# A list-scheduled transformer block on one core: the planner learns PSUM banks and a VectorE-GpSimd lock, norm1's gain goes into w_in, freed buffers are passed on, the second norm is done in halves, and the first MLP splits join the plan

## The chip, the cores and the metric

The kernel runs on one core of a Trainium2 chip. Its time is device microseconds of one execution; the time before is the median of three, 1164.03 us (1163.81 to 1168.68).

## What is computed

One block of a hybrid transformer in float32, on 1024 tokens of width 1024:

```python
h = rms_norm(x, norm1_g)
proj = h @ w_in                               # [1024, 1024] x [1024, 2560]
q, k, v, xl, gl = split(proj)                 # five parts of 512
q, k = rms_norm of each head (8 heads of 64), with q_norm_g, k_norm_g
attn = stick_breaking_attention(q, k, v)      # per 128 rows; a product of (1 - sigmoid z) over later keys
xl = causal_depthwise_conv(xl)                # 4 taps
lru = rg_lru(xl) * gelu(gl)                   # two 64x64 block gates, then a linear recurrence over time
x = x + concat(attn, lru) @ w_out             # [1024, 1024] x [1024, 1024]
h = rms_norm(x, norm2_g)
x = x + square(relu(h @ w_up)) @ w_down       # 1024 -> 4096 -> 1024
```

## The kernel before

**Products.** Every large product is three matmuls: each operand is split into a high part, rounded to fp32r, and a low part, the rest (high by a copy, low by a subtraction), and low x high, high x low and high x high are summed in PSUM. So each operand of TensorE passes two other engines first.

**Two stages.** The front holds everything up to the second norm, 0 to about 533 us of the profile. The MLP behind it multiplies 2x2 blocks with seven products in place of eight, in a sequence written out by hand (`up_group`, `down_group`, L980 is the helper that issues all of it); the change touches only its first few splits.

**The front's order** is not written by hand. `record_front` (L370 and on) records operations as `op(engine, cost in ns, function, reads, writes)`, grouped in units: X (transpose two 128-row tiles of x, `xt`, and split them into `hTh`, `hTl`), S (mean square of x), C (small vectors), W (load 128x256 blocks of w_in, `wrq`/`wrv`/`wrl`, and split them into `wq`, `wv`, `wl`), Q, V, L (projections, `pq`, `pv`, `pxl`, `pgl`, and what follows them: `ss`, `qv`, `rb` are the head norms), A and D (attention of a pair of heads and 256 rows: scores `z`, `G` the scan, `w` the weights, `pw` their transposes, `wt` their split, `av` the product), B (blocks of w_out, `ro`, split into `wo`), M (blocks of the mixer's output, `rm`, split into `mx`), O and U (product `po`, added to `x1`), H (second norm: transpose x1, `ht`, times norm2_g into `h2`; squares `jh`). The string `ORDER` gives the units' priorities. `Plan.schedule` then runs an event-driven list schedule over PE, DVE, ACT, POOL and SP with the given costs, and what it finds is the order in which each engine's instructions are issued (`Pinned` holds them to it; all are issued from L859). Its costs before are round: 900 ns for a VectorE low part of 128x512, 1400 to 1500 ns for a GpSimd operation of that shape; it lets any two engines read one PSUM bank at once, and lets VectorE and GpSimd run beside each other.

**Buffers.** `COUNT` gives the slots per tag. `CLOSES`/`OPENS` say which tags end before others begin, since they take the same memory: x1, wo, mx and r2 (the buffers of B, M, O and U) open only when the last user of w, wr, lg, f, hT, rsb and bd is done; h2 opens when attention is done. In program order, the loads of B50 and B40 come first in `ORDER` but wait for that.

**The hand-over.** After the plan `mlp_head()` issues the splits of the first MLP operands (`m0b` from h2, `sb` from w_up), and the first four MLP products are not held to program order (`PINNED = 4`).

Of the kernel before, what the change touches and what calls it, by code (L numbers as in the profile page):

```python
# [10 lines left out]
F32 = mybir.dt.float32  # L11
F32R = mybir.dt.float32r
# [8 lines left out]
P = 128  # L21
# [29 lines left out]
PTAGS = ("z", "pd", "pw", "av")  # L51

MM = {512: 227, 384: 173, 256: 117, 128: 109}
WIN = 3413.0
KEEP = {"PE": 0, "DVE": -77, "ACT": -95, "POOL": -40, "SP": 0}


def dve(n):
    return 210 + 0.93 * n


def dve2(n):
    return 230 + 1.45 * n


def act(n):
    return 185 + 0.82 * n


def gps(n):  # L70
    return 350 + 1.95 * n


class V:
    def __init__(self, plan, tag, name):
        self.plan, self.tag, self.name = plan, tag, name
        self.wr, self.rd, self.real = {}, {}, None
        self.slot, self.ops, self.allocs = None, {}, []
        self.left = None
# [10 lines left out]
class Op:  # L90
    __slots__ = ("eng", "cost", "fn", "deps", "succ", "prio", "set", "grp", "nd", "ready", "start", "end", "unit", "kb", "what", "tiles", "n", "as_", "ae", "work", "closes")


class Plan:
    def __init__(self):
        self.ops, self.queue, self.unit = [], {}, 0
        self.groups = {}
# [4 lines left out]
    def op(self, eng, cost, fn, r=(), w=(), set=None, grp=None, kb=0, what="", work=None):  # L102
        o = Op()
        o.work = work
# [26 lines left out]
        for acc in r:  # L131
            v, sub = acc if isinstance(acc, tuple) else (acc, None)
            v.rd.setdefault(sub, []).append(o)
            v.ops[o] = 1
        deps.pop(o, None)
# [29 lines left out]
    def schedule(self):  # L165
# [3 lines left out]
        dma_free = 0.0  # L169
# [35 lines left out]
        while len(done) < n:  # L205
# [68 lines left out]
            else:  # L274
                o.end = s + cost
# [4 lines left out]
            for q in o.succ:  # L280
                lat = 0 if q.eng == e and e != "SP" else 150 if q.eng == "POOL" else 50
# [6 lines left out]
            for v in o.tiles:  # L288
                v.left -= 1
                v.end = max(v.end, o.end)  # L290
                if not v.left:
                    k, q = nxt[v.tag], self.queue[v.tag]
                    if k < len(q):
                        nxt[v.tag] = k + 1
                        alloc(q[k], v.slot, v.end + 50)
            for k in o.closes:
                left[k] -= 1
                late[k] = max(late[k], o.end)
                if not left[k]:
                    for tag in OPENS[k]:  # L300
# [17 lines left out]
def record_front(plan, E, order):  # L318
# [4 lines left out]
    bd = V(plan, None, "bd")  # L323
# [8 lines left out]

    def const0():
        E.grow = plan.tile("lg", "grow")
        g = E.grow
        op("SP", 0, lambda: E.sp.dma_start(g[:NT, 0:P], E.norm1_g.rearrange("o (c p) -> (o c) p", p=P)), w=[g], kb=4)
        pg = plan.tile("pd", "pg1")
        op("PE", 260, lambda: E.pe.transpose(pg[:, 0:NT], g[:NT, 0:P], E.ident[:NT, :NT]), r=[g], w=[pg], what="gain")
        op("DVE", 170, lambda: E.dve.tensor_copy(E.gain1, pg[:, 0:NT]), r=[pg], w=[gain1], what="gain")

    def const1():
        vr = plan.tile("lg", "vrow")

        def loads():
            E.sp.dma_start(vr[0:16, 0:P], E.conv_w.rearrange("o k (c p) -> (o k c) p", p=P))
            for i, v in enumerate((E.conv_b, E.b_rg, E.b_ig, E.lam)):
                E.sp.dma_start(vr[16 + 4 * i:20 + 4 * i, 0:P], v.rearrange("o (c p) -> (o c) p", p=P))
            E.sp.dma_start(vr[32:40, 0:P], E.norm2_g.rearrange("o (c p) -> (o c) p", p=P))
            for i, v in enumerate((E.q_norm_g, E.k_norm_g)):
                for h in range(2):  # L350
                    E.sp.dma_start(vr[40 + i:41 + i, HD * h:HD * h + HD], v)
        op("SP", 10, loads, w=[vr], kb=30)
        pv = plan.tile("pd", "pv")
        op("PE", 260, lambda: E.pe.transpose(pv[:, 0:42], vr[:42, 0:P], E.ident[:42, :42]), r=[vr], w=[pv], what="vec")
        op("DVE", 200, lambda: E.dve.tensor_copy(E.vec, pv[:, 0:42]), r=[pv], w=[vec], what="vec")
        op("DVE", 200, lambda: E.dve.scalar_tensor_tensor(E.gcol, E.vec[:, 40:41], 1.0 / math.sqrt(HD), E.vec[:, 41:42], op0=ALU.mult, op1=ALU.mult),
           r=[vec], w=[gcol])
        lm = lambda: E.vec[:, 28:32]
        ta, tb, tc_ = (V(plan, None, n) for n in ("ta", "tb", "tc"))
        op("DVE", 200, lambda: E.dve.tensor_scalar_mul(E.t_a, lm(), -1.0), r=[vec], w=[ta])  # L360
        op("DVE", 200, lambda: E.dve.tensor_tensor(E.t_b, lm(), E.t_a, op=ALU.max), r=[vec, ta], w=[tb])
        op("ACT", 200, lambda: E.act.activation(E.t_b, E.t_b, AF.Sigmoid, scale=-1.0), r=[tb], w=[tb], set="sig")
        op("DVE", 200, lambda: E.dve.tensor_scalar(E.t_c, E.t_b, -1.0, 2.0, op0=ALU.mult, op1=ALU.add), r=[tb], w=[tc_])
        op("DVE", 200, lambda: E.dve.reciprocal(E.t_c, E.t_c), r=[tc_], w=[tc_])
        op("DVE", 200, lambda: E.dve.tensor_tensor(E.t_b, E.t_b, E.t_c, op=ALU.mult), r=[tb, tc_], w=[tb])
        op("DVE", 200, lambda: E.dve.tensor_tensor(E.t_c, E.t_b, E.t_b, op=ALU.mult), r=[tb], w=[tc_])
        nt = 10
        op("DVE", 200, lambda: E.dve.tensor_scalar(E.sp_, E.t_c, 2.0 / (2 * nt + 1), 2.0 / (2 * nt - 1), op0=ALU.mult, op1=ALU.add), r=[tc_], w=[sp])
        for n in range(nt - 2, -1, -1):
            op("DVE", 220, lambda: E.dve.tensor_tensor(E.sp_, E.sp_, E.t_c, op=ALU.mult), r=[sp, tc_], w=[sp])  # L370
# [7 lines left out]
        def bdz():  # L378
            E.gps.memset(E.bd, 0.0)
# [960 lines left out]
```

## Time and profile before

| what | value |
|---|---|
| median of three runs | 1164.03 us |
| the profiled execution | 1168.66 us, span 1166.9 us, mean granted TensorE clock 0.983 |
| TensorE busy | 1113.8 us, 95% of the span |
| VectorE busy | 811.0 us |
| ScalarE busy | 614.3 us |
| GpSimd busy | 534.8 us |
| DMA | 116.65 MB, mean 100 GB/s |

Engines: PE is TensorE's matmul, PEld its weight load, DVE VectorE, ACT ScalarE, POOL GpSimd, SP the engine that issues most DMAs. In the page's second part a digit is a slice's busy share in tenths, in 40 slices of 29.2 us. Rows of the timeline give start (us), length (us), the instruction (output <- inputs, partitions x elements), how many were merged, and in brackets the idle time in front of it and what ended it. Rows of the groups give count, busy us, mean ns of one, and idle time in front. A wait row gives who waited for whom, us, times, longest. A window row gives each engine's busy time, the granted clock (1.00 is full), the DMA share and GB/s.

### The profile page before, as it was taken

Reading aid. Unit: us, or ns where it says so; the run is one execution under the profiler, and the core shown is the slowest. Engines: PE = TensorE matmul, PEld = TensorE weight load, DVE = VectorE, ACT = ScalarE, POOL = GpSimd, SP = SyncE. Lnnn points to the kernel's source line nnn. Section 1 sums busy time; section 2 is a strip of 40 time slices with the busy share of each in tenths; the row PEclk is TensorE's granted clock in tenths of the full one; section 3 lists DMA queues with packets and bytes.
Section 4 is the critical chain, followed back from the end, with each engine's and each line's share of the span. In section 5 each row is a group of like instructions: output and inputs, shape, how many; then the busy total and the mean of one; then the engine's idle time right before and its main releaser. Section 6 shows DMA issues by size and latency. Waiting matters only on the chain.

```text
span 1166.9 us, 15585 instructions
## 1 busy us (share of the span) xinstructions
PE 1113.8 (95%) x5546; PEld 913.2 (78%) x5546; DVE 811.0 (70%) x1074; ACT 614.3 (53%) x1098; POOL 534.8 (46%) x447
## 2 busy tenths in 40 slices
PE   5899999999999699998999999999999999999998
PEld 4788877898777578876878888778887888887787
DVE  4457648743873698434866778997768667889965
ACT  5655756844865565446722774333456237643341
POOL 2455565625755744201244465852203534668431
PEclk9999999999999699998999999999999999999999
DMA  5101111111111740014343323554533433245644
GB/s 182 49 19 42 51 41 41 34 45 41 37 37 42 280 153 10 1 37 136 110 132 112 99 67 106 166 187 133 185 97 109 135 109 99 73 134 157 197 157 158
DMA packets 78293, 116.65 MB, mean 100 GB/s; under 512 B 8792, under 2 KB 28808, under 8 KB 78216
## 3 DMA queue, kind: packets, MB, share of 16 engines
q1 hardware_dynamic: 75912, 111.47, 30.5%
q10 hardware_dynamic: 2304, 4.20, 1.0%
q8 instruction: 43, 0.70, 0.3%
q14 instruction: 34, 0.28, 0.1%
HBM read 103.57 MB, written 12.06 MB: 99 GB/s over the span
## 4 chain that ended last, share of the span: by engine, by line
PE 70%; DVE 14%; ACT 7%; issue 4%; POOL 4%; DMA 1%; SPq 0%; ACTq 0%; POOLq 0%; DVEq 0%
PE p L980 25%; PE pa L980 12%; PE pb L980 5%; PE po L859 5%; DVE G L859 5%; PE pq L859 5%; PE pc L980 4%; PE pv L859 4%; PE pgl L859 2%; PE av L859 2%; PE pxl L859 2%; PE pw L859 2%; PE z L859 1%; POOL r_ea L980 1%; ACT hTh L859 1%
## 5 line engine op out<-in xcount | busy, mean ns | idle before, releaser
L859 POOL TENSOR_TENSOR w<-w,G 128x1024 f32<-128x1024 f32 (+3 forms) x48 | 76.0, 1593 | 65.5 <-ACT w L859 28.4
L980 DVE TENSOR_TENSOR U<-p,U 128x512 f32<-128x512 f32 x80 | 55.1, 689 | 63.9 <-PE p L980 63.8
L980 POOL TENSOR_TENSOR U<-U 128x512 f32<-128x512 f32 x48 | 69.0, 1445 | 65.7 <-ACT U L980 42.3
L980 PE MATMUL p<-m0t,st 128*128 128x512 f32 x384 | 89.7, 392 | 2.3 <-DVE U L980 2.3
L980 PE MATMUL p<-m1t,st 128*128 128x512 f32 x384 | 89.8, 392 | 1.2 <-DVE U L980 1.2
L859 PE MATMUL pq<-hTh,wq 128*128 128x512 f32 x256 | 89.7, 411 | 0.0
L859 PE MATMUL po<-wo,mx 128*128 128x512 f32 x336 | 86.5, 402 | 0.9 <-DVE x L859 0.9
L980 PEld LDWEIGHTS p<-m0t,st 128*128 128x128 f32 x384 | 71.9, 188 | 18.7 <-issue 2.7
L980 PEld LDWEIGHTS p<-m1t,st 128*128 128x128 f32 x384 | 71.9, 188 | 17.7 <-ACT sb L980 1.6
L980 POOL TENSOR_TENSOR r_sb<-r_sb,r_sa 128x512 f32<-128x512 f32 x16 | 23.7, 1480 | 115.1 <-DMA r_sb<-in_w_up_dram 100.9
L980 PE MATMUL p<-m0b,sb 128*128 128x512 f32 x288 | 69.6, 400 | 4.4 <-ACT h L859 4.4
L859 PEld LDWEIGHTS po<-wo,mx 128*128 128x128 f32 x336 | 61.9, 191 | 13.7 <-DVE x L859 1.3
L859 DVE TENSOR_TENSOR wt<-pw,wt 128x512 fp32r<-128x512 f32 (+1 forms) x80 | 50.1, 627 | 31.2 <-ACT wt L859 30.7
L859 DVE TENSOR_TENSOR_SCAN G<-G,K 128x769 f32<-128x769 f32 (+3 forms) x32 | 65.1, 2044 | 8.4 <-ACT G L859 8.4
L980 PEld LDWEIGHTS p<-m0b,sb 128*128 128x128 f32 x288 | 55.7, 194 | 16.9 <-ACT h L859 4.7
L980 PE MATMUL p<-m1b,sb 128*128 128x512 f32 x288 | 67.3, 391 | 0.0
L859 PEld LDWEIGHTS av<-wt,v 128*128 128x128 f32 x320 | 47.3, 191 | 24.5 <-DVE wt L859 15.0
L859 ACT CAST wt<-pw 128x512 fp32r<-128x512 f32 (+1 forms) x80 | 43.4, 543 | 43.3 <-PE pw L859 42.5
L859 PE MATMUL av<-wt,v 128*128 128x256 f32 (+1 forms) x320 | 54.1, 291 | 10.3 <-DVE wt L859 6.9
L980 PEld LDWEIGHTS p<-m1b,sb 128*128 128x128 f32 x288 | 54.1, 188 | 11.8
L980 ACT ACTIVATE U<-U 128x512 f32<-128x512 f32 x96 | 58.9, 630 | 5.6 <-DVE U L980 2.6
L859 PEld LDWEIGHTS pq<-hTh,wq 128*128 128x128 f32 x256 | 48.6, 190 | 10.3 <-issue 0.5
(234 smaller groups left out, 2922.5 us busy)
## 6 DMA issues: line engine op xcount, KB each, us to landing
ro<-in_w_out_dram SPq DMA_DIRECT2D x20, 256.0 KB
x<-in_x_dram SPq DMA_DIRECT2D x8, 512.0 KB
wrq<-in_w_in_dram SPq DMA_DIRECT2D x32, 128.0 KB
wrl<-in_w_in_dram SPq DMA_DIRECT2D x32, 128.0 KB
x<-in_x_dram SPq DMA_DIRECT2D x16, 256.0 KB
r_a<-in_w_up_dram SPq DMA_DIRECT2D x16, 256.0 KB
r_b<-in_w_up_dram SPq DMA_DIRECT2D x16, 256.0 KB
r_sa<-in_w_up_dram SPq DMA_DIRECT2D x16, 256.0 KB
```

The costliest lines, as they stand in the source:

```text
L859: self.last = tc.keep_in_program_order(getattr(self.eng, op)(*args, **kw))
L980: ins = getattr(self.eng, op)(*args, **kw)
```

## The change

**The planner.** `ALT`, a table found beforehand, moves named operations of a unit to another engine (weight products `w`, low parts of q, k, mx, wo, and LRU products, GpSimd to VectorE; some `h2` copies, ScalarE to VectorE). Operations on PSUM tags depend on the last operation of another engine on the same bank. An operation with `port` set (all GpSimd operations but memsets, and VectorE ones with operands in SBUF) waits for one shared lock. Costs and latencies are new numbers, for instance 668 ns on VectorE and 1275 on GpSimd for a 128x512 low part, and `155 + 2.07 n` for a scan of n. `ORDER` is another string.

**norm1_g folded.** X units evacuate whole banks without the gain; W units multiply by it instead, ScalarE for the high part and VectorE (one scalar_tensor_tensor) for every low part; before, 5 of 8 low parts were GpSimd's. All small vectors come as one array `vecs`, in one DMA; before, eleven.

**Buffers.** w (now two halves of 512 floats) and f, once their own queue is used up, hand their slots on to a new tag u, which holds ro, rm, wo, mx and the squares' scratch; lg lies in x1's memory; 38 more u slots open when hT closes.

**Second norm in halves.** H0 and H1 transpose and scale 512 rows each instead of 256 in four units; the squares are units N of their own.

**First MLP splits** are units Y (two w_up blocks) and Z (eight blocks of h2); `mlp_head` is gone and the MLP is held to program order from its first product.

```diff
-COUNT = dict(w=10, wr=3, ..., lg=11, f=9, qk=5, ..., wo=14, mx=8, r2=8, h2=1, s2=4)
+COUNT = dict(wr=3, ..., ot=2, lg=15, w=9, f=8, u=0, qk=4, ..., h2=1, s2=8, mv=8, st=2, ra=2, uu=38)
-CLOSES = (("w", "wr", "lg", "f", "hT", "rsb", "bd"), ("A", "G", "wt", "ob", "ot", "qk", "v", "sm"))
-OPENS = (("x1", "wo", "mx", "r2"), ("h2",))
+CLOSES = (("wr", "lg", "hT", "rsb", "bd"), ("A", "G", "wt", "ob", "ot", "qk", "v", "sm", "zb"))
+OPENS = (("x1",), ("h2", "mv", "st", "ra"))
+ALT = {"A03": (16, 20,), "A10": (7, 11,), ..., "H0": (7, 8, 12,), "H1": (4, 7, 15, 16,), ...}
...
+        if alt is not None:
+            self.flex.append((self.uname, self.inunit, o))
+            if self.inunit in ALT.get(self.uname, ()):
+                eng, cost, port = alt
+            f, e = fn, eng
+            fn = lambda: f(e)
+        o.port = eng == "POOL" if port is None else port
...
+        for acc in list(r) + list(w):
+            v, sub = acc if isinstance(acc, tuple) else (acc, None)
+            if v.tag in PTAGS:
+                for b in banks(v, sub):
+                    for e, d in v.bank.items():
+                        if e[0] == b and e[1] != eng:
+                            deps[d] = 1
...
-                o.end = s + cost
+                b = s
+                if o.port:
+                    b = max(s, port)
+                    port = b + cost
+                o.end = b + cost
...
                 if not v.left:
                     k, q = nxt[v.tag], self.queue[v.tag]
+                    if k >= len(q) and v.tag in ("w", "f"):
+                        k, q = nxt["u"], self.queue["u"]
+                        slot = f"{v.tag}{slot}"
...
     def xunit(tp):
-                    E.act.mul(E.hTh[:, kc, 256 * tp:256 * tp + 256], src(), E.gain1[:, kc:kc + 1])
+                    E.act.copy(E.hTh[:, k, o], src())
-                    E.dve.scalar_tensor_tensor(E.hTl[:, kc, o], src(), E.gain1[:, kc:kc + 1], E.hTh[:, kc, o].bitcast(F32), ...)
+                    E.dve.tensor_tensor(E.hTl[:, k, o], src(), E.hTh[:, k, o].bitcast(F32), op=ALU.subtract)
...
     def wunit(key):
-            op("ACT", 410, lambda wr=wr, wt=wt: E.act.copy(wt[:, 0], wr[:]), ...)
-            if kc % 8 in E.dvelo:
-                op("DVE", 640, ... lo(E.dve, ...)
-            else:
-                op("POOL", 850, ... lo(E.gps, ...)
+            op("ACT", 490, lambda ...: E.act.mul(wt()[:, 0], wr[:], E.vec[:, kc:kc + 1]), r=[wr, vec], ...)
+                E.dve.scalar_tensor_tensor(wt()[:, 1], wr[:], E.vec[:, kc:kc + 1], wt()[:, 0].bitcast(F32), ...)
+            op("DVE", 415, lw, r=[wr, vec, (u, 0)], w=[(u, 1)], port=True, ...)
...
+    def hunit(g):
+        for b in range(4):
+            z = plan.tile("z", f"ht{g}{b}")
+            for j in range(2):
+                ... four transposes of x1 rows 4g to 4g + 3 into z[:, j]
+            for j in range(2):
+                def ev(e, kc=kc, j=j, z=z):
+                    a = (H2[:, kc, 512 * g:512 * g + 512], z[:, j], E.vec[:, 40 + kc:41 + kc])
+                    E.act.mul(*a) if e == "ACT" else E.dve.tensor_scalar_mul(*a)
+                op("ACT", 690, ev, ..., alt=("DVE", 690, False))
...
-    mlp_head()
+    nload, pinned = 2, True
```

What the planner then issues, at three places. ScalarE at the program's start, before: x rows are squared into scratch (`jk`), then four copies of 256 columns each empty a pair of PSUM banks (`xt`).

```order
L859 ACTIVATE jk_203,ssx_204<-x_164 128x1024
L859 ACTIVATE jk_209,ssx_204<-x_166 128x1024
L859 ACTIVATE hTh<-xt_206,gain_90 128x256 x4
L859 ACTIVATE hTh<-xt_223,gain_90 128x256 x4
L859 CAST wq_251<-wrq_177 128x256
L859 CAST wq_258<-wrq_181 128x256
L859 CAST wq_263<-wrq_183 128x256
L859 ACTIVATE hTh<-xt_247,gain_90 128x256 x4
L859 ACTIVATE hTh<-xt_275,gain_90 128x256 x4
```

The same place now: two copies of 512 columns per pair of banks, a square between them, and the w_in blocks with the gain `vec`.

```order
L912 ACTIVATE x_83,ssx_195<-x_165 128x1024
L912 CAST hTh<-xt_189 128x2x256 x2
L912 ACTIVATE x_83,ssx_195<-x_167 128x1024
L912 CAST hTh<-xt_204 128x2x256 x2
L912 ACTIVATE wq_236<-wrq_179,vec 128x256
L912 ACTIVATE wq_240<-wrq_181,vec 128x256
L912 ACTIVATE wq_246<-wrq_183,vec 128x256
L912 CAST hTh<-xt_228 128x2x256 x2
L912 ACTIVATE x_83,ssx_266<-x_185 128x1024
L912 CAST hTh<-xt_252 128x2x256 x2
```

So 32 copies of 256 columns became 16 of 512 (2x256 in the second form), and the rows come in another sequence of tiles.

TensorE where the last projection chain (`pq`) ends and the output product (`po`) begins, before: behind the last `pq` stand scores, head norms (`rb`, `ss`) and two small attention units.

```order
L859 MATMUL pq_3772<-hTh,wq_3604 128x512
L859 MATMUL z_3819<-k_2975,q_2888 128x128 x6
...
L859 MATMUL rb_3841<-ident,sq_3779 128x128 x4
L859 MATMUL ss_3848<-ones_97,sq_3837 128x2 x4
L859 MATMUL z_3864<-k_3112,q_2888 128x512 x6
...
L859 MATMUL rb_3883<-ident,sq_3837 128x128 x4
...
L859 MATMUL av_3929<-wt_3951,v_2831 128x256 x2
...
L859 MATMUL z_4001<-k_3897,q_3853 128x128 x6
...
L859 MATMUL po_4041<-wo_3963,mx_3985 128x512 x3
```

The same place now:

```order
L912 MATMUL pq_3775<-hTh,wq_3563 128x512
L912 MATMUL rb_3831<-ident,sq_3735 128x128 x4
L912 MATMUL pw_3854<-ident,w_3542 128x128
...
L912 MATMUL z_3878<-k_3860,q_3783 128x128 x6
L912 MATMUL z_3879<-k_3860,q_3783 128x256 x6
...
L912 MATMUL av_3920<-wt_3873,v_2749 128x256 x2
...
L912 MATMUL po_3939<-woh_3818,mxl_3905 128x512
```

One head norm and one small attention step are left between the last `pq` and the first `po`; the rest of the last head norms moved behind the first `po` chains, and the attention units that stood here moved ahead of the chain.

The engine that empties the second norm's transposes (`ht`) into h2 at the end of the front was ScalarE before, 256 columns at a time, and then split them (`m0b`).

```order
L859 ACTIVATE h_5084<-ht_5187,vec 128x256 x4
L859 ACTIVATE h_5084<-ht_5200,vec 128x256 x4
L859 ACTIVATE h_5084<-ht_5212,vec 128x256 x4
L859 ACTIVATE h_5084<-ht_5225,vec 128x256 x4
L859 ACTIVATE jh_5250,ssh_5108<-x_3910 128x1024
L859 ACTIVATE h_5084<-ht_5238,vec 128x256 x4
L980 CAST m0b_5310<-h_5084 128x512
```

Now it is VectorE, in whole banks:

```order
L912 TENSOR_TENSOR m0b_5166<-h_5044,m0b_5166 128x512
L912 TENSOR_TENSOR m0b_5174<-h_5044,m0b_5174 128x512
L912 TENSOR_TENSOR x_83<-po_5157,x_83 128x512
L912 TENSOR_SCALAR h_5044<-ht_5181,vec 128x512 x2
L912 TENSOR_SCALAR h_5044<-ht_5192,vec 128x512 x2
L912 TENSOR_SCALAR ssh_5097<-ssh_5097 128x4
L912 TENSOR_SCALAR h_5044<-ht_5205,vec 128x512 x2
L912 TENSOR_SCALAR h_5044<-ht_5218,vec 128x512 x2
```

Of the 24 copies that stood in the last stretch before, eight remain behind the last `po` addition (`x<-po`), and the splits of the first half stand ahead of it. `ALT` names three `h2` copies of H0 and four of H1 for VectorE; in the built order all sixteen are VectorE's, because `e`, which the wrapped function reads when it is issued, has meanwhile been used again as the loop variable of the bank rule in `op`.

More of the change, by code (lines that the diff above doesn't have):

```diff
@@ L78, in __init__ @@
         self.slot, self.ops, self.allocs = None, {}, []
-        self.left = None
+        self.bank = {}
     def get(self):
@@ L90, with banks @@
 class Op:
-    __slots__ = ("eng", "cost", "fn", "deps", "succ", "prio", "set", "grp", "nd", "ready", "start", "end", "unit", "kb", "what", "tiles", "n", "as_", "ae", "work", "closes")
+    __slots__ = ("alt", "eng", "cost", "fn", "deps", "succ", "prio", "set", "grp", "nd", "ready", "start", "end", "unit", "kb", "what", "tiles", "n", "as_", "ae", "work", "closes", "port", "base", "idx")
+def banks(v, sub):
+    return (0, 1) if v.tag == "z" and sub is None else (sub,) if v.tag == "z" else (0,)
 class Plan:
@@ L299, in schedule @@
                 if not left[k]:
+                    if not k:
+                        q = self.queue["u"]
+                        a = nxt["u"]
+                        nxt["u"] = min(len(q), a + COUNT["uu"])
+                        for i in range(a, nxt["u"]):
+                            alloc(q[i], f"uu{i - a}", late[k] + 50)
                     for tag in OPENS[k]:
@@ L341, in const1, with on @@
-    def const1():
[L342 to L358, printed above, removed]
+    def on(e):
+        return {"DVE": E.dve, "POOL": E.gps, "ACT": E.act}[e]
@@ L623, in st @@
+            op("POOL", 1285, lambda e_, u=u, y=y: mult(e_, y[:, 0:512], u[:, 0:512], y[:, 0:512]), r=[u, y], w=[y], what=f"hy{nm}", alt=("DVE", 668, True))
             def st(y=y, ch=int(nm[1])):
@@ L646, in bound @@
                         E.gps.memset(G[:, 2 * kn + 1:2 * kn + 2], 1.0)
-                    op("POOL", 200, bound, w=[(G, "b")], what=f"gm{p}{c}")
+                    op("POOL", 200, bound, w=[(G, "b")], what=f"gm{p}{c}", port=False)
             def burst(steps=steps, zs=zs):
@@ new lines, in record_front, with split, yunit @@
+    NS = {}
+    E.first = {}
+    def split(v, src, r, name):
+        op("ACT", 628, lambda: E.act.copy(v[:, 0], src()), r=r, w=[(v, 0)], what=f"{name}h")
+        op("DVE", 668, lambda e: lo(on(e), v[:, 1], src(), v[:, 0]), r=r + [(v, 0)], w=[(v, 1)], what=f"{name}l", port=True, alt=("POOL", 1275, True))
+    def yunit(n):
+        r, s = plan.tile("ra", f"r_a0{n}"), plan.tile("st", f"sb11{n}")
+        op("SP", 0, lambda: E.sp.dma_start(r[:], E.w_up[0, n]), w=[r], kb=256, what="w_up")
+        split(s, lambda: r[:], [r], "st")
+        E.first["st", n] = s
@@ new lines, in zunit, with nunit, sq @@
+    def zunit(k):
+        for u in range(4):
+            m = plan.tile("mv", f"m0b{k + 1}1{u}")
+            split(m, lambda u=u: H2[:, 4 * k + u, 0:512], [(H2, (4 * k + u, 0))], "mv")
+            E.first[f"0b{k + 1}1", u] = m
+    def nunit(t):
+        if t // 4 not in NS:
+            NS[t // 4] = plan.tile("s2", f"ssh{t // 4}")
+        ss, jk = NS[t // 4], plan.tile("u", f"jh{t}")
+        def sq():
+            E.act.activation(jk[:].bitcast(BF16), E.x1[:, t, :], AF.Square, accum_out=ss[:, t % 4:t % 4 + 1])
+        op("ACT", 1060, sq, r=[a for n in range(2) for a in (X1[t, n], XF[t, n])], w=[jk, (ss, t % 4)], what=f"ssh{t}")
@@ L829, with kernel @@
 @with_exitstack
-def kernel(ctx, tc, x, norm1_g, w_in, conv_w, conv_b, w_rg, b_rg, w_ig, b_ig,
-                             lam, q_norm_g, k_norm_g, w_out, norm2_g, w_up, w_down, out):
+def kernel(ctx, tc, x, vecs, w_in, w_rg, w_ig, w_out, w_up, w_down, out):
     nc = tc.nc
```

431 lines of the change are left out of this document (214 added, 217 removed), and 18 rows, old and new, of tables (ALT, ORDER).

## The prediction

> **What bounds the kernel now.** I read the page's totals and slices first, then the time by stage, then what TensorE waits for.
>
> ```profile
> span 1166.9 us, 15585 instructions
> PE 1113.8 (95%) x5546; PEld 913.2 (78%) x5546; DVE 811.0 (70%) x1074; ACT 614.3 (53%) x1098; POOL 534.8 (46%) x447
> PE   5899999999999699998999999999999999999998
> PEclk9999999999999699998999999999999999999999
> ```
>
> TensorE is the bound, and no product is added or removed, so only its idle time, its slow-clock time and matmuls that stand waiting can be won. They lie at three places: the first slices, slice 13 (380 to 408 us, the clock falls too), and slice 18. The stages (core 0; time, then busy us of PE, PEld, DVE, ACT, POOL, then clock, DMA share, GB/s):
>
> ```profile
> 0.00:40.00 40.00, 24.86 (x108) 19.03 (x108) 22.05 (x76) 24.88 (x58) 8.79 (x25) 1.00 0.46 152
> 40.00:350.00 310.00, 301.47 (x1840) 252.28 (x1841) 192.90 (x250) 191.20 (x340) 170.62 (x175) 0.99 0.13 39
> 350.00:400.00 50.00, 39.84 (x211) 31.72 (x210) 25.01 (x33) 29.03 (x49) 28.79 (x22) 0.80 0.37 124
> 400.00:500.00 100.00, 99.00 (x569) 82.54 (x568) 72.04 (x90) 53.74 (x94) 40.73 (x41) 1.00 0.23 79
> 500.00:533.00 33.00, 26.50 (x137) 21.62 (x136) 10.19 (x21) 19.76 (x48) 1.76 (x3) 0.97 0.22 67
> 533.00:1167.00 634.00, 622.11 (x2688) 506.02 (x2687) 488.82 (x607) 295.68 (x515) 284.14 (x184) 0.99 0.42 130
> ```
>
> Of 53.1 us of idle TensorE, 41 lie in the front's 533 us. One MLP product takes 622.11 / 2688 = 0.23 us; that is my price of a 512-column product everywhere. The waits (us in total, times, longest):
>
> ```profile
> PE av L859 <- DVE wt L859: 6.9, 6, 2.9
> PE xt L859 <- ACT hTh L859: 6.5, 4, 2.5
> PE rb L859 <- ACT sq L859: 5.2, 3, 2.0
> PE p L980 <- ACT h L859: 4.4, 1, 4.4
> PE p L980 <- DVE U L980: 3.6, 2, 2.3
> PE xt L859 <- DMA x<-in_x_dram: 3.3, 2, 2.4
> ```
>
> All but the fifth are in the front. That one, with 12 us of idle time after 533 us, belongs to a sequence the change leaves alone: its terms are 0, give or take 2 us for the other split of the `sb` ring and for holding the first four products to program order.
>
> **Part 1, the start: 8 us less (2 to 12).** ScalarE and VectorE empty the transposed x in turns:
>
> ```profile
> 6.40 1.06 ACT L859 ACTIVATE jk<-x 128x1024 bf16<-128x1024 f32 x1 [0.18 <-DMA x<-in_x_dram]
> 7.78 0.47 ACT L859 ACTIVATE hTh<-xt,gain 128x256 fp32r<-128x256 f32 x1 [0.23 <-PE xt L859]
> 9.04 0.48 ACT L859 ACTIVATE hTh<-xt,gain 128x256 fp32r<-128x256 f32 x1 [0.78 <-PE xt L859]
> 9.55 0.48 DVE L859 SCALAR_TENSOR_TENSOR hTl<-xt,gain,hTh 128x256 fp32r<-128x256 f32 x1 [1.59 <-ACT hTh L859]
> 10.06 0.47 ACT L859 ACTIVATE hTh<-xt,gain 128x256 fp32r<-128x256 f32 x1 [0.55 <-DVE hTl L859]
> 15.27 0.88 DVE L859 SCALAR_TENSOR_TENSOR hTl<-xt,gain,hTh 128x256 fp32r<-128x256 f32 x2 [0.54 <-ACT hTh L859]
> 21.12 0.80 PE L859 MATMUL pq<-hTh,wq 128*128 128x512 f32 x1
> ```
>
> At 9.04, 9.55 and 10.06 each engine starts where the other ends: two readers of one bank never overlap. The first pair of tiles takes from 7.78 to about 15.7, the first product runs at 21.12, and by 40 us TensorE has issued 108 instructions, 64 of them transposes and two for vectors: 42 products. Afterwards a whole bank goes through at a time, one engine on each of two banks. The prices of a 512-column copy and of a VectorE operation that reads PSUM, and of a w_in high part, are these groups' (count, busy us, mean ns, idle before):
>
> ```profile
> L859 ACT CAST wt<-pw 128x512 fp32r<-128x512 f32 x48 | 28.1, 585 | 31.2 <-PE pw L859 30.8
> L859 DVE TENSOR_TENSOR x<-po,x 128x512 f32<-128x512 f32 x24 | 16.5, 687 | 19.5 <-PE po L859 17.7 <-DMA ro<-in_w_out_dram 1.7
> L859 ACT CAST wq<-wrq 128x256 fp32r<-128x256 f32 x32 | 11.9, 405 | 5.0 <-DMA wrq<-in_w_in_dram 3.0 <-PE pgl L859 1.8
> ```
>
> A pair then costs 4 x 0.69 + 0.59 = 3.4 us in place of 8. ScalarE becomes the limit: up to the eighth block of the first chain it has six squares (1.06, and about 0.2 to read the sum), 12 copies (0.59) and eight blocks. A block costs 0.405 without the gain and 0.47 with it, by the `hTh` rows of the same shape. That is 7.6 + 7.1 + 3.8 = 18.5 us from about 5.1 on: 23.6. By then 18 products are out; the other 16.4 us hold 16.4 / 0.23 = 71. So 89 products by 40 us against 42, 47 x 0.23 = 10.8 us. I take 8: the last two blocks' loads stand on SP behind x loads that wait for free tiles. The low end is the case that these come 6 us late, the high end is 10.8 and a little of the DMA wait (split loads let the transposes begin on half rows). The gain in the 56 later blocks adds 56 x 0.07 = 3.9 us to ScalarE, hidden: it was busy 319 of the front's 533 us by the rows above. The one vector DMA takes ten issues off SP, and is 0 here.
>
> **Part 2, the hole at 373 us: 11 us less (3 to 16).**
>
> ```profile
> 371.00 4.25 SPq L859 DMA_DIRECT2D ro<-in_w_out_dram  x2
> 372.80 0.39 PE L859 MATMUL pq<-hTh,wq 128*128 128x512 f32 x1
> 395.18 2.75 PE L859 MATMUL po<-wo,mx 128*128 128x512 f32 x6
> 425.83 2.54 DMA ro<-in_w_out_dram
> ```
>
> The last chain of hT ends at 373.2; w_out could be loaded only then (the issue at 371.00 stands 4.25 us), and the first `po` runs 22 us later. Between them stand head norms and small attention steps that wait for each other. The stretch 350 to 400 loses 10.2 us idle and, at clock 0.80, 0.2 x 39.84 = 8.0 us: 18. In the new order the last chain is Q31, whose norms stand behind the first `po`; the first loads of w_out go into freed f slots ahead of the chain's end, and two small steps are left between. The first `po` needs blocks 4 and 5 of w_out and of the mixer. The last of these is the sixth load in SP's order: about 1.5 us of issues after the chain's end, 2.5 us to land (the 425.83 row), three copies and three low parts at 0.6 to 0.7 in two engines' queues, with other work between: 7 to 8 us. TensorE has about 3 us of work there. So 4.5 us of idle time stay, and about 2 at a low clock: 18 - 6.5 = 11.5, I take 11. Low end: the loads queue behind each other, 14 us and its clock; high end: only 2 us stay. By the Trainium skill (TensorE: Matmul & The Clock Gate, What's actually happening) the clock falls to half after an idle window of about 3.4 us. The row of 0.80 around the waits agrees, and by it a remaining hole under that length would keep the full clock and make this term 13.
>
> **Part 3, the hand-over: 5.5 us less (2 to 8).**
>
> ```profile
> 519.57 0.60 PE L859 MATMUL ht<-ident,x 128*128 128x128 f32 x4
> 532.58 1.65 PE L980 MATMUL p<-m0b,sb 128*128 128x512 f32 x3 [4.42 <-ACT h L859]
> ```
>
> From the last `po` to the first MLP product 13.0 us pass: 48 transposes, 24 copies on ScalarE, then splits. Now 32 transposes remain behind the last `po`, 16 of them waiting for banks, and VectorE adds `po` to x1 and empties eight banks, all eight, whatever `ALT` says: about 8 x 0.69 + 0.3 = 5.8 us until the bank that the first product takes is free. The splits stand ahead. 16 more transposes go in line before, 16 x 0.11 = 1.8 us. 13.0 - 5.8 - 1.8 = 5.4. If VectorE arrives late, 2; if the first product's bank is free earlier, 8. Copies shared with ScalarE, as the planner believes, would be worth some 2 us more.
>
> **Part 4, the rest of the front: 8 us less (10 more to 22 less).** VectorE and GpSimd block each other:
>
> ```profile
> 32.46 0.16 DVE L859 TENSOR_SCALAR sp__95<-sp__95 128x4 f32<-128x4 f32 x1
> 32.99 0.42 DVE L859 TENSOR_TENSOR wq<-wrq,wq 128x256 fp32r<-128x256 f32 x1
> 33.27 0.75 POOL L859 TENSOR_TENSOR wq<-wrq,wq 128x256 fp32r<-128x256 f32 x1 [5.31 <-ACT wq L859]
> 33.32 0.73 DVE L859 TENSOR_SCALAR sp__95<-sp__95 128x4 f32<-128x4 f32 x1
> ```
>
> The same operation on four columns takes 0.16 us alone and 0.73 beside GpSimd, ending when GpSimd ends (34.02 against 34.05). The Trainium skill (SBUF — State Buffer, SBUF: two separate sides) calls that port pair an exclusive lock, and these rows agree. It costs:
>
> ```profile
> L859 DVE TENSOR_TENSOR wo<-ro,wo 128x512 fp32r<-128x512 f32 x10 | 12.5, 1278 | 0.6 <-ACT wo L859 0.6
> L859 DVE TENSOR_TENSOR wl<-wrl,wl 128x256 fp32r<-128x256 f32 x12 | 10.1, 846 | 4.6 <-ACT wl L859 4.3 <-issue 0.3
> L859 POOL TENSOR_TENSOR w<-w,G 128x1024 f32<-128x1024 f32 x24 | 49.6, 2068 | 27.6 <-DVE G L859 16.0 <-ACT w L859 11.6
> ```
>
> 10 x (1278 - 687) + 12 x (846 - 420) ns = 11 us of waiting in these two groups alone. Against that, VectorE gets more work. By the new order: 64 w_in low parts where 30 were (+14), 16 x 0.69 in place of 32 x 0.48 for hTl (-4), 23 attention products at 0.4 to 1.2 (+21; up to 2.07 on GpSimd), 24 LRU and q, k operations of 512 columns (+16), `h2` (+11), others (+3): 61 us on an engine busy 322 us in the front, 383 of some 500. GpSimd loses more than 100. The lock is held for less time in all, and the planner now knows it, the banks and the prices, so TensorE's order meets its operands more often. What there is to win: 9.5 us idle (40 to 350 and 400 to 500), and matmuls that stand waiting though they count as busy. I take 8. Upper end: idle time and both groups' waiting all go. Lower end: a sixth of the new VectorE work falls on TensorE's path with no gain. One rule speaks against such moves: the Trainium skill (Perfetto Trace Analysis, Optimizing Scalar/DVE Operations) says that moving work between these two may not help, because they share the port; no row here shows a moved operation, and by it the sum would be 24.5.
>
> **Sum.** 8 + 11 + 5.5 + 8 = 32.5 us: the profiled execution would take 1168.7 - 32.5 = 1136.2 us. It stood 4.6 us over the median; the same gain from 1164.0 is **1131.5 us**. The ends are 17 - 20 = -3 and 58; all four at one end is unlikely, so this case alone is 1116 to 1148.
>
> **The rivals.** *All of it works*: parts 1 to 4 at their upper ends, 45 to 58 us, 1106 to 1119. For it: costs taken from rows that fit. Against: VectorE at 77% has little room for lateness. *The moves do nothing and part 2 is at its low end*: 14 to 22 us, 1142 to 1150; parts 1 and 3 are changes of structure and stay. *The waits only move* (a hole opens wherever VectorE is late, and gives back 27 to 32 us): 1158 to 1164, no change. *Slower*: VectorE becomes what TensorE waits for. The 61 us of new work stand in its queue in front of `wt`, which `av` waits for already (6.9 us, the longest wait). It decides when over 32.5 / 61 = 53% of it falls on the path; at 70% the time is 1164 + 42.7 - 32.5 = 1174. Against it: GpSimd's operations it replaces were slower and blocked VectorE too.
>
> **How the numbers follow.** Forecast 0.62, all of it 0.14, moves do nothing 0.10, waits only move 0.05, slower 0.09. A difference of 0.5%, 5.8 us, is about what a measurement of this kernel can tell from no change. The first three are faster, 0.86; same 0.05; slower 0.09. The range runs from the lower end of "all of it" to above "moves do nothing": 1106 to 1156.
>
> **What would show it.** Right: the first `pq` at 12 to 14 us and dense products from 24 us; no slice under 8 tenths around the first `po`, which follows the last `pq` by about 8 us; the first MLP product 6 us after the last `po`; VectorE low parts of 512 near 0.67 us. Wrong: `av <- DVE wt` or waits for VectorE grown over 20 us in all, idle slices in the middle of the front, or the MLP stage off 634 us by more than 3.

## The result and the profile after

The changed kernel takes **1129.64 us** (median of four, 1128.52 to 1132.01), the kernel before on the same chip 1165.52 us (four, 1163.81 to 1168.68): a ratio of 0.969 (95% interval 0.966 to 0.972). The forecast was 1131.5. The profiled execution of the changed kernel took 1128.52 us, 40.1 less than that of before, which stood 3.1 over its median.

The page's totals and slices of the changed kernel:

```profile
span 1126.7 us, 15511 instructions
PE 1100.5 (98%) x5545; PEld 901.3 (80%) x5545; DVE 840.8 (75%) x1164; ACT 604.7 (54%) x1050; POOL 411.0 (36%) x350
PE   7999999999998999999999999999999999999998
PEclk9999999999999999999999999999999999999999
```

TensorE is busy for 98% of the span in place of 95%, and no slice is at a lower clock. VectorE gained 30 us of work and GpSimd lost 124. The stages (time, then busy us of PE, PEld, DVE, ACT, POOL, then clock, DMA share, GB/s):

```profile
0.00:40.00 40.00, 32.03 (x173) 25.98 (x173) 22.95 (x78) 27.35 (x55) 8.57 (x22) 1.00 0.50 152
40.00:340.00 300.00, 297.59 (x1859) 250.16 (x1859) 222.74 (x329) 203.21 (x347) 74.32 (x98) 1.00 0.14 43
340.00:400.00 60.00, 56.65 (x314) 45.68 (x314) 42.77 (x58) 35.16 (x64) 30.75 (x32) 1.00 0.56 198
400.00:480.00 80.00, 79.34 (x448) 66.40 (x445) 56.42 (x78) 39.81 (x69) 13.52 (x13) 1.00 0.08 27
480.00:494.00 14.00, 11.35 (x73) 9.54 (x71) 11.88 (x20) 7.08 (x14) 2.61 (x2) 1.00 0.40 128
494.00:1127.00 633.00, 623.53 (x2688) 503.58 (x2688) 484.06 (x603) 292.06 (x506) 281.18 (x184) 1.00 0.41 129
```

For the third row, the same 60 us of the kernel before:

```profile
340.00:400.00 60.00, 49.84 (x263) 39.67 (x262) 29.32 (x41) 35.75 (x60) 32.45 (x25) 0.83 0.34 112
```

TensorE stood idle for 10.2 us there and lost 0.17 x 49.84 = 8.5 us to the clock; now 3.35 us and nothing. What TensorE waits for now:

```profile
PE xt L912 <- DMA x<-in_x_dram: 4.5, 3, 3.5
PE p L1041 <- DVE rs L912: 1.6, 1, 1.6
PE av L912 <- DVE wt L912: 1.6, 4, 0.7
```

`av <- wt` fell from 6.9 to 1.6 us, though VectorE has more to do; the longest wait left is for the first rows of x.

The start, a ScalarE copy, VectorE's subtraction and the first product:

```profile
7.05 1.05 ACT L912 CAST hTh<-xt 128x512 fp32r<-128x512 f32 x2
8.13 1.29 DVE L912 TENSOR_TENSOR hTl<-xt,hTh 128x512 fp32r<-128x512 f32 x2 [5.12 <-ACT hTh L912]
9.04 1.07 ACT L912 CAST hTh<-xt 128x512 fp32r<-128x512 f32 x2
12.35 0.47 PE L912 MATMUL pq<-hTh,wq 128*128 128x512 f32 x1
```

The last `pq`, the steps behind it and the first `po`, and SP's loads of w_out ahead of it:

```profile
319.56 0.34 SPq L912 DMA_DIRECT2D ro<-in_w_out_dram  x1
349.07 4.04 SPq L912 DMA_DIRECT2D ro<-in_w_out_dram  x3
353.68 0.39 PE L912 MATMUL pq<-hTh,wq 128*128 128x512 f32 x1
355.38 0.52 PE L912 MATMUL pw<-ident,w 128*128 128x128 f32 x3 [0.87 <-DVE f L912]
359.02 0.48 PE L912 MATMUL po<-woh,mxl 128*128 128x512 f32 x1
```

Four loads of w_out are issued before the last `pq`; in the kernel before it was one. From the last `pq` to the first `po` 5.3 us pass in place of 22.4, with no wait over 0.9 us. The hand-over, TensorE and VectorE:

```profile
487.09 0.39 PE L912 MATMUL po<-woh,mxdh 128*128 128x512 f32 x1
488.48 2.72 DVE L912 TENSOR_SCALAR h<-ht,vec 128x512 f32<-128x512 f32 x4
490.02 1.06 PE L912 MATMUL ht<-ident,x 128*128 128x128 f32 x8 [0.80 <-DVE h L912]
491.18 2.72 DVE L912 TENSOR_SCALAR h<-ht,vec 128x512 f32<-128x512 f32 x4
494.04 3.20 PE L1041 MATMUL p<-m0b,sb 128*128 128x512 f32 x13 [1.64 <-DVE rs L912]
```

Eight copies stand in VectorE's queue behind the last `po`, then the last step of the second norm (`rs`), for which TensorE waits 1.64 us. The first MLP product comes 6.95 us after the last `po`, before 13.2.

Against the terms of the prediction, in the profiled executions:

| term | predicted | found | from |
|---|---|---|---|
| start | 8 (2 to 12) | 8.3 | 78 products of the first chains issued by 40 us, before 42: 36 x 0.23 |
| hole | 11 (3 to 16) | 15.3 | 18.6 - 3.35, the two rows 340 to 400 |
| hand-over | 5.5 (2 to 8) | 4.5 | 13.2 - 6.95 - 1.8 for the 16 transposes that went ahead |
| rest of the front | 8 (-10 to 22) | 10.4 | what is left of 38.5, by which the first MLP product is earlier (532.58 to 494.04) |
| MLP | 0 (2 either way) | 1.6 | 1166.9 - 532.58 = 634.3 against 632.7 |

The last term is no gain. Two runs below leave the MLP as it was before, and take 631.7 and 631.1 us for it; over all runs below the profiles have 631.1 to 637.8 us. So a few us of a total can lie in the MLP, which no run's edit is aimed at, and small differences are read from the front.

### The profile page after: what moved, and what is told of

Its sections match the earlier page's. It is cut to its first block, busy times and chain, and to the rows that moved or that the text cites. A ratio compares the mean times of both kernels' runs of the same rounds, so it can differ in the third digit from the quotient of the medians.

```text
span 1126.7 us, 15511 instructions
## 1 busy us (share of the span) xinstructions
PE 1100.5 (98%) x5545; PEld 901.3 (80%) x5545; DVE 840.8 (75%) x1164; ACT 604.7 (54%) x1050; POOL 411.0 (36%) x350
## 4 chain that ended last, share of the span: by engine, by line
PE 84%; DVE 7%; issue 3%; DMA 2%; ACT 2%; POOL 1%; SPq 0%; ACTq 0%; POOLq 0%; DVEq 0%
PE p L1041 26%; PE pa L1041 12%; PE pq L912 8%; PE po L912 7%; PE pb L1041 5%; PE pc L1041 4%; PE pv L912 4%; PE pxl L912 4%; PE pgl L912 3%; PE av L912 3%; PE z L912 3%; PE pw L912 3%; DMA x<-in_x_dram 1%; PE ss L912 1%; POOL r_ea L1041 1%
## 5 line engine op out<-in xcount | busy, mean ns | idle before, releaser
L1041 POOL TENSOR_TENSOR r_sb<-r_sb,r_sa 128x512 f32<-128x512 f32 x16 | 22.4, 1403 | 109.9 <-DMA r_sb<-in_w_up_dram 96.3
L912 POOL TENSOR_TENSOR w<-w,G 128x1024 f32<-128x1024 f32 (+3 forms) x25 | 38.5, 1550 | 63.9 <-ACT w L912 23.2
L912 DVE TENSOR_TENSOR_SCAN G<-G,K 128x769 f32<-128x769 f32 (+3 forms) x32 | 49.6, 1565 | 4.8 <-ACT G L912 4.7
L912 PE MATMUL pq<-hTl,wq 128*128 128x512 f32 x128 | 50.2, 392 | 0.4 <-DVE hTl L912 0.4
L1041 PE MATMUL pc<-mgc,sgc 128*128 128x512 f32 x192 | 47.1, 394 | 3.0 <-ACT sga L1041 3.0
```

Source lines behind the costliest of these rows:

```text
L912: self.last = tc.keep_in_program_order(getattr(self.eng, op)(*args, **kw))
L1041: ins = getattr(self.eng, op)(*args, **kw)
```

## The experiments

The theory is the prediction's: four terms, two of them changes of structure (whole banks at the start, early loads of w_out), and moved work that pays because GpSimd is slower and blocks VectorE. The rivals were that the moves do nothing, that VectorE is the bound, and that it is the string of priorities alone. All times are medians, and each run was timed beside the kernel before.

**1. The moved operations back on GpSimd, in the same order.**

```diff
             f, e = fn, eng
+            if self.uname[0] not in "HYZ":
+                e = "POOL"
             fn = lambda: f(e)
```

> The changed kernel with one edit: the 67 operations that the table moves from GpSimd to VectorE outside the first MLP splits (23 weight products, 15 LRU products, 9 low parts of q and k, 20 low parts of w_out and the mixer; 52 us of VectorE by the planner's costs, 100 us on GpSimd) are issued on GpSimd again, at the same place in the same order. Theory (the moves are worth most of the 9.6 us that the rest of the front won): 8 us or more over the changed kernel's 1129.6, so 1138 to 1150, with TensorE's waits for GpSimd or for what stands behind it up. Rival 1 (a shared port, so it does not matter which of the two does the work): 1127 to 1133. Rival 2 (VectorE is what holds the front up, so taking 52 us off it helps): under 1126.

Measured: 1141.35 us, ratio 0.979 (0.977 to 0.982), 11.7 over the changed kernel. The front of this run, then of the changed kernel:

```profile
0.00:505.00 505.00, 481.04 (x2858) 401.68 (x2859) 321.60 (x496) 313.13 (x544) 230.87 (x233) 0.99 0.22 69
```

```profile
0.00:494.00 494.00, 476.97 (x2857) 397.75 (x2857) 356.76 (x561) 312.62 (x544) 129.78 (x166) 1.00 0.22 71
```

35 us of VectorE against 101 of GpSimd, and the front is 10.7 us shorter with the work on VectorE. The theory holds; both rivals fall. For GpSimd itself TensorE waits only 1.8 us in this run. The largest wait that the changed kernel doesn't have is for ScalarE's squares of the head norms; that these come late because of GpSimd is not shown.

```profile
PE rb L914 <- ACT sq L914: 4.5, 2, 2.9
```

**2. The h2 copies shared as the planner has them.** The inner loop takes the name `e` from the operation, so all 16 copies ran on VectorE; renamed, 9 run on ScalarE.

```diff
-                    for e, d in v.bank.items():
-                        if e[0] == b and e[1] != eng:
+                    for k, d in v.bank.items():
+                        if k[0] == b and k[1] != eng:
```

> The changed kernel with a loop variable renamed, so that 9 of the 16 copies of h2 run on ScalarE, where the planner put them, and not all 16 on VectorE; nothing else moves. Theory (after the last po VectorE's queue decides when the first MLP product can start: 6.95 us from the last po to it): the stretch falls by 1 to 2 us, the time to 1127.5 to 1129. Rival (the end of the second norm, whose last step TensorE waits 1.6 us for, decides): no change of the stretch within 0.4 us.

Measured: 1128.56 us, ratio 0.968 (0.967 to 0.970), not to be told from the changed kernel. The last `po` starts at 485.80, and its hand-over:

```profile
487.69 1.05 ACT L912 ACTIVATE jh<-x 128x1024 bf16<-128x1024 f32 x1
489.27 1.84 ACT L912 ACTIVATE h<-ht,vec 128x512 f32<-128x512 f32 x3 [0.44 <-DVE h L912]
491.14 1.41 DVE L912 TENSOR_SCALAR h<-ht,vec 128x512 f32<-128x512 f32 x2 [1.83 <-PE ht L912]
492.70 4.55 PE L1041 MATMUL p<-m0b,sb 128*128 128x512 f32 x19 [1.59 <-DVE rs L912]
```

6.90 us, as before (6.95): ScalarE squares the last rows of x1 first, its copies come after that, and VectorE stands idle for 1.83 us. The stretch did not fall, so the theory fails here, and the rival fits: the wait for `rs` is 1.59 us with half of the copies off VectorE, 1.64 with all of them on it. That the square is to blame is read from the rows and was not tried.

**3. Slots handed on, in the plan, only when the last chain of hT has ended.**

```diff
                         slot = f"{v.tag}{slot}"
+                        if left[0]:
+                            held_u.append(slot)
+                            continue
...
                             alloc(q[i], f"uu{i - a}", late[k] + 50)
+                        for slot in held_u:
+                            if nxt["u"] < len(q):
+                                nxt["u"] += 1
+                                alloc(q[nxt["u"] - 1], slot, late[k] + 50)
```

> The changed kernel, but the slots of w and f are handed to w_out's and the mixer's tiles only when the last chain of hT has ended, as all of these tiles were before; the planner lays out the order anew with this. Theory (early loads of w_out are what closed the hole between the last pq and the first po): that stretch grows from 5.3 us to 12 us or more, and the kernel is 6 to 14 us slower, 1136 to 1144. Rival (the hole came from head norms and small attention steps that waited for each other, and the order alone removed it): the stretch stays under 8 us and the time within 4 us of 1129.6.

Measured: 1135.97 us, ratio 0.975 (0.972 to 0.979), 6.3 over the changed kernel. The last `pq` starts at 354.26; then:

```profile
342.65 0.86 SPq L919 DMA_DIRECT2D ro<-in_w_out_dram  x2
354.68 0.81 SPq L919 DMA_DIRECT2D ro<-in_w_out_dram  x2
360.99 0.79 PE L919 MATMUL z<-k,q 64*128 64x384 f32 x6 [1.75 <-ACT w L919]
364.16 1.65 PE L919 MATMUL z<-k,q 64*128 64x512 f32 x6 [2.38 <-ACT w L919]
367.72 0.78 PE L919 MATMUL po<-woh,mxl 128*128 128x512 f32 x1
```

```profile
350.00:370.00 20.00, 14.56 (x81) 11.24 (x81) 9.83 (x16) 12.98 (x25) 6.48 (x7) 0.84 0.67 238
```

The stretch is 13.5 us in place of 5.3, and the clock falls again. So the early hand-on holds about 6 to 8 of the 15.3 us. This is rough: the edit delays the loads in the plan, and on the chip two of them still go out 11.6 us ahead of the last `pq` (four did in the changed kernel). What TensorE waits for longest in the stretch is ScalarE's `w` (2.38 and 1.75 us), in attention steps that the new plan puts there. The rest is put down to what stands no longer between chain and `po`, since even so the stretch is 9 us shorter than before; no run takes that apart.

**4. x emptied in quarters.**

```diff
-            for j in range(2):
-                kc = 4 * b + 2 * j
+            for i in range(4):
+                kc, j = 4 * b + i, i // 2
...
-                op("ACT", 604, hi, r=[(z, j)], ...)
+                op("ACT", 405, hi, r=[(z, j)], ...)
...
-            if v.tag in PTAGS:
+            if v.tag in PTAGS and what[:2] != "hT":
                 for b in banks(v, sub):
```

> The changed kernel with the transposed x emptied in pieces of 256 columns, four copies on ScalarE and four subtractions on VectorE for a pair of banks, and the planner believing for these alone that both engines may read one bank at once, as before; no gain in them. Theory (taking turns within a bank cost the start its time): the eight pieces go in turns at 0.40 to 0.47 us, a pair takes about 6 us in place of 3.4, 78 products by 40 us become 50 to 62, and the time is 4 to 7 us longer, 1133.5 to 1137. Rival (x's loads and squares set the pace of the start): under 2 us longer.

Measured: 1134.46 us, ratio 0.973 (0.972 to 0.975), 4.8 over the changed kernel, in the theory's range, but not for its reason: 81 products are out by 40 us, not 50 to 62. The pieces go in turns only for the first pairs; later ScalarE runs ahead of VectorE:

```profile
7.57 0.37 ACT L908 CAST hTh<-xt 128x256 fp32r<-128x256 f32 x1 [0.49 <-DVE hTl L908]
13.44 1.65 ACT L908 CAST hTh<-xt 128x256 fp32r<-128x256 f32 x5 [0.49 <-DVE hTl L908]
18.25 2.30 ACT L908 CAST hTh<-xt 128x256 fp32r<-128x256 f32 x8
```

The front ends 2.5 us later, lost between 40 and 100 us; the MLP of this profile takes 2.9 us more. So in this order the form of the evacuation isn't what makes the start.

**5. The kernel before with whole banks alone.**

```diff
-            for j in range(4):
+            for j in (0, 2):
                 kc = 4 * b + j
...
-                op("ACT", 494, hi, r=[(z, j), gain1], ...)
+                op("ACT", 604, hi, r=[(z, j), (z, j + 1)], ...)
```

> The kernel before with one edit: the transposed x is emptied a whole bank at a time, two copies of 512 columns on ScalarE and two subtractions on VectorE for a pair of banks; norm1's gain is left out of these two (and so of the result), since a bank holds two columns of gain. Order string, planner and loads stay as before. Theory (ScalarE and VectorE took turns in each bank, and that set the pace of the first 21 us): the first pq moves from 21.1 us to 15 to 17, and the time falls by 4 to 7 us. Rival (the order of the first units and the vector loads in SP's queue set it): the first pq stays after 19 us, and the time within 2 us of the kernel before.

Measured: 1162.52 us, ratio 0.998 (0.997 to 0.999), 2.4 less than before. The first `pq` moves from 21.12 to 17.26, between the two expectations, but by 40 us there are 48 products in place of 42: 1.4 us of the 8.3. TensorE then stands for 3.3 us ahead of the transposes of the last two tiles of x, a wait for which the profile names no cause; the second half of x is loaded from 15.9 us on. The front is 3.4 us shorter in all.

**9. The same with one load of the vectors.** (The numbers are those of the order in which they ran.)

```diff
-        def loads():
-            E.sp.dma_start(vr[0:16, 0:P], E.conv_w...)
...
-        op("SP", 10, loads, w=[vr], kb=30)
+        op("SP", 0, lambda: E.sp.dma_start(vr[0:42, 0:P], E.vecs[8:50]), w=[vr], kb=25)
```

> The kernel before with x emptied in whole banks (norm1's gain left out there, as in the run with whole banks alone) and the ten loads of small vectors replaced by one. The run with whole banks alone had its first pq at 17.3 us, 49 products of the first chains by 40 us and its front 3.4 us shorter; its x loads of the second half were issued at 15.9 us, behind the vectors' loads. Theory (those issues stand in front of the x loads and so were not free, other than the prediction had it): x loads by 11 us, 58 products or more by 40 us, 2 to 4 us off. Rival (free, as the prediction had it): 49 to 52 products, within 1 us of the run with whole banks alone, 1162.5.

Measured: 1154.58 us, ratio 0.991 (0.989 to 0.993), 7.9 less than with whole banks alone. SP's queue in the kernel before, then in this run:

```profile
4.58 0.44 SPq L859 DMA_DIRECT2D vrow<-in_conv_w_dram  x1
9.20 1.49 SPq L859 DMA_DIRECT2D vrow<-in_q_norm_g_dram  x2
14.19 1.02 SPq L859 DMA_DIRECT2D x<-in_x_dram  x2
SPq L859 <- DMA x<-in_x_dram: 3.0, 3, 1.0
```

```profile
4.56 0.44 SPq L850 DMA_DIRECT2D vrow<-in_vecs_dram  x1
11.54 0.34 SPq L850 DMA_DIRECT2D x<-in_x_dram  x1
SPq L850 <- PE xt L850: 5.1, 2, 3.0
```

(The last row of each is SP's longest wait in its first 16 us.) In the kernel before, SP stands 3.0 us in its queue for the first loads of x to land, between the issues of the vectors. With one load it gets to the second half of x early, and waits there until TensorE's transposes have freed a tile.

71 products are out by 40 us, 23 more than with whole banks alone (48; the 49 in the expectation is one too many): 23 x 0.23 = 5.3 us of the start. The ten issues were not free; the theory holds and is more than it expected. The front is 8.7 us shorter, 3.4 of it behind 40 us, in an order that the planner laid out anew.

**6. The string of before in the changed kernel.**

```diff
 ORDER = (
-    "X2 C0 Wq0 X3 X0 X1 C2 S2 ... N6 Z0 H1 "
+    "B50 C0 X0 Wq0 B40 X1 C1 C2 S1 ... O70 N7 Z0 H1 "
 ).split()
```

> The changed kernel with the string of unit priorities of before (the new units put in where their work stood); the planner with its rules and prices, the moves and the buffers stay as in the change, and the planner lays the work out from this string. Theory (the four terms are changes of structure, so most of them survives another string: start and buffers at least): 1135 to 1150. Rival (the string found for this planner is what makes the gain; any other one gives it back): 1155 to 1170.

Measured: 1156.94 us, ratio 0.994 (0.992 to 0.996), 27 over the changed kernel: the rival's side, with the table of moves left as it was. Start (73 products by 40 us), hole (5.0 us from `pq` to `po`) and hand-over (7.5 us) are there. What is lost is the rest of the front. TensorE's waits for VectorE sum to 20.9 us in place of 10.8, those for ScalarE to 14.7 in place of 4.4, and the mean clock is 0.988 in place of 1.000. The longest:

```profile
PE av L907 <- DVE wt L907: 8.8, 5, 5.3
```

**7 and 8. A string searched with and without the two rules.** Both searches start from the string of run 6; the strings and tables found stand in place of `ORDER` and `ALT`. The second has

```diff
-                        if k[0] == b and k[1] != eng:
-                            deps[d] = 1
+                        pass
...
-                if o.port:
+                if False:
```

> The changed kernel (with the h2 copies shared as planned), its string and table of moves found anew by a search of 800 s from the string of the run above, with the planner's rules on the lock and the banks on. Theory (the rules and prices fit the chip, so an order that is found with them holds on it): 1132 to 1142, no wait of TensorE for VectorE or GpSimd over 3 us at a place. Rival (the rules are beside the point): no better than the search without them.

> As the run above, the same search from the same string for the same time, but with both rules off: the planner lets VectorE and GpSimd run beside each other and two engines read one bank. Theory (knowing the lock and the banks is what lets TensorE's order meet its operands): 10 us or more slower than the search with rules, 1145 to 1165. Rival (any searched order does as well): within 5 us of the search with rules.

Measured: 1133.8 us with the rules, ratio 0.973 (0.972 to 0.975); 1149.97 without, ratio 0.988 (0.986 to 0.990). The wait for the attention's low parts, with, then without:

```profile
PE av L901 <- DVE wt L901: 2.6, 6, 0.9
```

```profile
PE av L900 <- DVE wt L900: 11.3, 11, 2.8
```

With lock and banks known, the same search from the same start found an order that is 16 us faster; both sides lie in the theory's ranges, and the run with the rules has no wait for VectorE over 3 us. But there is one search of each kind, the two rules were switched off together, and run 12 shows that the string alone can move 15 us; how far two searches of one kind differ was not measured. VectorE is as busy in both fronts (351 and 358 us), so it is when its work comes and not how much there is.

**10. Low parts of w_in back on GpSimd.**

```diff
             def lw(wr=wr, wt=wt, kc=kc):
+                if kc in DVELO:
                     E.dve.scalar_tensor_tensor(...)
+                else:
+                    lo(E.gps, wt()[:, 1], wr[:], wt()[:, 0])
```

> The changed kernel with five of eight low parts of w_in (40 of 64) on GpSimd again, as before, at the same place in the order; they leave out the gain there. Theory (a move from VectorE to GpSimd costs, since GpSimd takes longer and holds the port meanwhile): 3 to 9 us slower, 1133 to 1139. Rival (VectorE is short of room, so 17 us less on it helps): under 1128.

Measured: 1132.9 us, ratio 0.972 (0.971 to 0.974), 3.3 over the changed kernel. The first MLP product is as early as in the changed kernel (494.17 us), and the MLP of this profile took 5 us longer. So the number is in the theory's range, but the front shows no price: in this order the low parts on GpSimd had cover. (Run 1 left these on VectorE, so its 11.7 us come from other moves.)

**11. All that can move on VectorE.**

```diff
             f, e = fn, eng
+            if self.uname[0] not in "HYZ":
+                e = "DVE"
             fn = lambda: f(e)
```

> The changed kernel with the other 55 operations that could be moved from GpSimd to VectorE (25 weight products, 9 LRU products, 7 low parts of q and k, 14 of w_out and the mixer; 50 us more on VectorE) moved too, at the same place in the order. Theory (VectorE has that room only where the table says; elsewhere its queue is what TensorE meets): 3 to 12 us slower, 1133 to 1142, with waits for VectorE up. Rival 1 (a move always pays): 1121 to 1128. Rival 2 (VectorE becomes the bound): over 1150.

Measured: 1135.94 us, ratio 0.975 (0.973 to 0.977), 6.3 over the changed kernel. The low parts of w_out in the changed kernel (14 on VectorE, 6 on GpSimd), then here:

```profile
L912 DVE TENSOR_TENSOR wol<-ro,woh 128x512 fp32r<-128x512 f32 x14 | 11.6, 828 | 3.6 <-ACT woh L912 3.6
L912 POOL TENSOR_TENSOR wol<-ro,woh 128x512 fp32r<-128x512 f32 x6 | 8.5, 1409 | 16.9 <-ACT woh L912 16.8
```

```profile
L914 DVE TENSOR_TENSOR wol<-ro,woh 128x512 fp32r<-128x512 f32 x20 | 13.6, 685 | 3.8 <-ACT woh L914 3.8
PE av L914 <- DVE wt L914: 3.5, 7, 0.8
```

With GpSimd nearly still, one takes 685 ns, beside a busier GpSimd 828, and 1278 in the kernel before. Yet the front ends 4.6 us later (of the 7.4 us by which the profile is longer, the other 2.8 lie in the MLP): each operation is quick, but more of them stand in one queue, and TensorE waits for `wt` seven times in place of four, 3.5 us in place of 1.6. The rest of the 4.6 us is not accounted for.

**12. Two neighbours of the string swapped.**

```diff
-    "B60 A00 R0 Wl0 Wq1 L00 L01 Q11 Q10 Wl1 ...
+    "B60 A00 R0 Wl0 Wq1 L00 L01 Q10 Q11 Wl1 ...
```

> The changed kernel with two neighbours of the string of priorities swapped (Q10 before Q11); the planner lays the work out anew. Theory (a list schedule hangs on its string, so that most of the rest of the front's gain is in the string): 5 to 20 us slower, lost in stretches far from the swap too. Rival (the rules and buffers carry it): within 4 us of 1129.6.

Measured: 1144.78 us, ratio 0.983 (0.981 to 0.985), 15 over the changed kernel. Two waits that come to 1.6 us there come to 11.5 here:

```profile
PE av L912 <- DVE wt L912: 6.8, 7, 1.9
PE pq L912 <- ACT x L912: 4.7, 1, 4.7
```

Start, hole and hand-over are unchanged to 1 us. So a run that lays the work out anew (3 to 9) carries some us of luck with its string; of those, the stretches named above and not the totals are the evidence.

## Why the prediction was right, step by step

**Sum.** 32.5 us were forecast and 34.4 found between the medians of 1164.03 and 1129.64. All four terms lie within their ranges. They add, with the MLP, to 40.1, since they come from the two profiled executions: that of before stood 4.6 us above its median of three, that of the changed kernel 1.1 below its own, and in which term this lies isn't known. (The lower end of the prediction's sum, -3, is 2 + 3 + 2 - 10.)

**Start: right size by luck, wrong step.** The step that failed is "the one vector DMA takes ten issues off SP, and is 0 here". It looked at the first pair of tiles, whose loads come ahead of the vectors', and not at the later x and w_in loads behind them in SP's queue. Run 9 shows 5.3 us for it, the luck of a new layout included, and run 5 only 1.4 for the whole banks, to which the prediction gave nearly all. The forecast of 89 products, with ScalarE as the limit, missed by 11. Turns within a bank are real, but the rows show VectorE's semaphore as what ScalarE waits for (0.55 us in the kernel before): they are waits of the program, and the order decides how often they bite (run 4).

**Hole: right, and larger.** The forecast left 4.5 us idle and 2 to the clock; 3.35 and 0 were left. Run 3 shows that handing slots on early carries about half of it. By the Trainium skill (TensorE: Matmul & The Clock Gate, What's actually happening) an idle window of about 3.4 us halves the clock, by which the prediction had this term at 13. The changed kernel agrees at this place, with waits under 1 us and clock 1.00. In run 3 the clock fell to 0.84 with no wait over 2.4 us, so there a stretch with little work (14.56 us busy of 20) did what the Trainium skill says there of an idle window.

**Hand-over: right size, its step not shown.** The prediction let VectorE's eight copies set the time, about 6 us; 6.95 were found, with the eight copies 0.69 us apart. But in run 2 VectorE has fewer of them and the stretch is 6.90, so they are not what alone decides. "Copies shared with ScalarE would be worth some 2 us more" was wrong: run 2 shows nothing within 0.1 us.

**Rest of the front: right size in part by luck; the chances hid how much hung on the string.** The moves pay 11.7 us in this order (run 1), as much as the whole term. The Trainium skill (Perfetto Trace Analysis, Optimizing Scalar/DVE Operations) says that moving work between the two may not help, because of the port. Here it helped, and the same work takes little more than half as long on VectorE (828 ns against 1409 for the low parts of w_out on GpSimd). Run 11 shows a limit: with 55 more of such moves the front ends 4.6 us later, though not for the port, since one then takes 685 ns. The order found with the rules is 16 us faster than the one found without (runs 7 and 8, one search each), and two swapped units cost 15. New VectorE work was put at 61 us; its busy time in the front rose from 322 to 357, 35 us. That it also waits less for the port is part of this (1278 to 828 ns for a low part of w_out); how much was not taken apart. That the low parts would take 0.67 us was too good: 0.83. The rival "waits only move" came closest to life in run 6: structure in place, old string, 1156.94.

## What to carry to other kernels

Where a list schedule sets the order, give it measured durations without contention and the resources that two engines share, then search its string again: in this kernel most of the gain hung on the order that was found so (runs 6 and 12). What the measured durations alone are worth was not tried. In an engine's queue of DMA issues, count what stands behind a row of small loads as well as what stands beside them. And test a mechanism in its stretch: a plan laid out anew can shift the total by 15 us for reasons of its own.

## What the runs showed that was not expected

- Replacing ten small loads by one was worth 5.3 us at the start of this kernel: the kernel before issues vectors, and then the gates' weights, from 4.58 to 14.19 us, with gaps in which SP waits for earlier loads to land, and four of eight x tiles come behind them.
- The clock falls (0.84 over 20 us of run 3) in a stretch whose longest wait is 2.38 us, and holds (1.00, 480 to 494 us of the changed kernel) over one of 1.64 us.
